# Gathered expert rows: nine buffers instead of four, rows emitted by TensorE's progress in the experts' pass, and a higher row pace beside the projections

## The chip, the cores and the metric

One core of one Trainium2 chip runs the whole program. The metric is the device time of one execution in microseconds (us). A profiled execution has a span, from its first to its last instruction, and a time of its own that is a little longer.

## The reference, cut to what matters

An encoder trunk of one layer runs over two token groups (256 and 1024 tokens, width 1024) with shared weights: retention and latent attention from one input projection, attention to 256 memory tokens, then a product-key expert layer and a last norm. The expert layer (PEER) is the part that the change touches: each token has 8 heads, each head picks 16 of 16384 experts, so 128 experts per token, and an expert is one row of U and one row of V (1024 floats each).

```python
def peer_ffn(xn, wq, sub_keys, U, V):
    def blk(xt):                                  # 128 tokens
        q = (xt @ wq).reshape(128, 8, 256)
        s1 = einsum('thd,hkd->thk', q[..., :128], sub_keys[0])
        s2 = einsum('thd,hkd->thk', q[..., 128:], sub_keys[1])
        v1, i1 = top_k(s1, 16); v2, i2 = top_k(s2, 16)
        cand = v1[..., :, None] + v2[..., None, :]        # 256 sums a head
        ts, sel = top_k(cand, 16)
        ids = take_along_axis(i1*128 + i2, sel)           # 128 experts a token
        g = softmax(ts)
        a = einsum('td,ted->te', xt, U[ids])
        return einsum('te,ted->td', g * gelu(a), V[ids])
y = rms_norm(x + peer_ffn(rms_norm(x, norm_ffn_w), ...), final_norm_w)
```

## The kernel before, in words

**Tiles and stages.** The 1280 tokens are ten tiles of 128. All work is written by one Python program, and a scheduler with a timeline model puts each engine's instructions in an order; on the chip every engine then runs its own list strictly in that order. The stages follow each other in time: the input projection with retention (`phase_a`), the first group's latent attention and its output, memory and query projections (`phase_m`, `phase_b` on tiles 0 and 1), the second group's latent attention (`phase_m`, to about 1110 us), `phase_b` on tiles 2 to 5 (to about 1440 us) and on tiles 6 to 9 (to about 1780 us), the gates (`gates`, to 2069 us), and the experts' pass (`dense`, to the end).

**Two ways to compute the experts.** Tiles 2 to 7 (`DENSE`) go through all 16384 experts on TensorE. `a_stage` loads blocks of U (`ur`), splits each into a high part on ScalarE (`uh`) and a low part on GpSimd (`ul`), and multiplies (PSUM tile `pa`, three matmuls a product); ScalarE takes the Gelu out of PSUM (`wr`), VectorE multiplies in the gates and makes the low part (`wl`); V blocks are loaded and split likewise (`vr`, `vh`, `vl`). `v_stage` multiplies into PSUM tile `pv` (two buffers) and VectorE adds it to `dacc`.

**Gathered rows.** Tiles 0, 1, 8 and 9 (`GATHER`) get only the rows they need. The generator `gather` makes, for each tile, 128 U rows and then 128 V rows. One row is an indirect DMA issued by GpSimd (line 1007) that brings 128 x 1024 floats, 0.5 MB, into a buffer of tag `grow`, of which there are four, and one VectorE instruction on it: for U a multiply with `x3` and a sum into one column of `a`, for V a multiply-add into `acc`. `banks` copies `x3` and `acc` into PSUM (tile `gps`) if the experts' pass has begun, and otherwise leaves them in SBUF (`gx`, `gacc`). 4 x 256 = 1024 rows in all.

**Where rows are put.** VectorE calls of the main work go through `Lead`, which remembers the last one as `anchor`; those of rows and of routing go through `Fill`, which gives each an ordering edge behind the current anchor: on VectorE it cannot come before it, and may come later. `tick(us)` is called beside each group of matmuls with its time at full rate. It adds that time, multiplied by a pace of `RHO`, to a debt, and takes steps of the routing generators (first) or of the gather generators until the debt is paid; a row pays 1.2 us. `RHO` has a pair (pace while routing is pending, pace of rows) for each of three stretches: the second group's attention and `phase_b`, the gates, the experts' pass. In the experts' pass the row pace is 0, and the rows left over are written after the whole pass, in the loop at the end of `run`, with the pass's beginning as anchor:

```python
            start = self.dense(sd)
            self.anchor = start
            while self.routing or self.gathering:
                self.step()
```

Of the kernel before, what the change touches and what calls it, by code (L numbers as in the profile page):

```python
# [10 lines left out]
F32 = mybir.dt.float32  # L11
F32R = mybir.dt.float32r
BF = mybir.dt.bfloat16
# [8 lines left out]
P = 128  # L22
D = 1024
# [23 lines left out]
NG = 3  # L47
O1_BY = "va"

RHO = ((0.75, 0.42), (0.5, 0.0), (0.9, 0.0))  # L50
LATE = 2


SYNC = mybir.DependencyInfo(mybir.DependencyClass.Sync, mybir.DependencyReason.DATA)
# [7 lines left out]
class Lead:  # L62


    def __init__(self, k):
        self.k = k
# [39 lines left out]
class K:  # L106
    def __init__(self, nc, tc, I, O, dbg=None):
        self.nc, self.tc, self.I, self.O = nc, tc, I, O
        self.dbg = dbg or {}
        self.n = 0  # L110
        self.routing, self.gathering = [], []
        self.keeps = []
        self.spare = ()
        self.routed = set()
        self.owed, self.rho = 0.0, (0.0, 0.0)
        self.gps = None
        self.anchor = None
        self.v, self.vf = Lead(self), Fill(self)

    def tick(self, us):  # L120


        rho = self.rho[0 if self.routing else 1]
        if self.rho is RHO[1] and self.routed.issuperset(DENSE):
            rho = 0.0
# [7 lines left out]
    def step(self, q=None):  # L133
        q = q or self.routing or self.gathering
        try:
            return next(q[0])
        except StopIteration:
            q.pop(0)
            return 0.0

    def pace(self, r, ins=None):
# [156 lines left out]
    def phase_a(self, sd):  # L298
# [3 lines left out]
        with ExitStack() as es:  # L302
# [20 lines left out]
            with ExitStack() as e2:  # L323
# [16 lines left out]
                for p in range(RH // 2):  # L340
# [9 lines left out]
                    for t in tiles:  # L350
# [12 lines left out]
                        nc.gpsimd.tensor_tensor(gg[t], gg[t], gw, ALU.mult)  # L363
                        if p and t == LATE:
                            finish()
# [620 lines left out]
    def gather(self, gp, sd, t):  # L986

        nc, I = self.nc, self.I
        v = self.vf

        def row():
            return gp.tile([P, D], F32, tag="grow", name=self.nm("grow"), bufs=4)
        ids = gp.tile([P, P], I32, tag="gids", name=self.nm("gids"), bufs=2)
        nc.sync.dma_start(ids, sd["ids"][t])
        g = gp.tile([P, P], F32, tag="gg", name=self.nm("gg"), bufs=2)
        nc.sync.dma_start(g, sd["g"][t])
        x3 = gp.tile([P, D], F32, tag="gx", name=self.nm("gx"), bufs=1)
        nc.sync.dma_start(x3, sd["x3"][t])
        fw = row()
        nc.sync.dma_start(fw, I["norm_ffn_w"].partition_broadcast(P))  # L1000
        v.tensor_tensor(x3, x3, fw, ALU.mult)
        x3 = self.banks(x3)
        a = gp.tile([P, P], F32, tag="ga", name=self.nm("ga"), bufs=2)

        def rows(src, s):
            u = row()
            nc.gpsimd.indirect_dma_start(out=u, out_offset=None, in_=src,  # L1007
                                         in_offset=bass.IndirectOffsetOnAxis(ap=ids[:, s:s + 1], axis=0))
            return u
        for s in range(P):  # L1010
            u = rows(I["peer_u"], s)
            junk = gp.tile([P, D], BF, tag="gj", name=self.nm("gj"), bufs=1)
            v.scalar_tensor_tensor(junk, u, 1.0, x3, ALU.mult, ALU.mult, accum_out=a[:, s:s + 1])
            yield 1.2
        nc.scalar.activation(a, a, AF.Gelu)
        v.tensor_tensor(a, a, g, ALU.mult)
        acc = gp.tile([P, D], F32, tag="gacc", name=self.nm("gacc"), bufs=1)
        nc.sync.dma_start(acc, sd["x2"][t])
        out, acc = acc, self.banks(acc)
        for s in range(P):  # L1020
            u = rows(I["peer_v"], s)
            v.scalar_tensor_tensor(acc, u, a[:, s:s + 1], acc, ALU.mult, ALU.add)
            yield 1.2
        w = row()
        nc.sync.dma_start(w, I["final_norm_w"].partition_broadcast(P))
        self.finish(gp, t, acc, w, gp.tile([P, D], BF, tag="gj", name=self.nm("gj"), bufs=1), out)

    def banks(self, x):

# [184 lines left out]
    def run(self):  # L1214
        nc, tc, I = self.nc, self.tc, self.I
        with ExitStack() as es:
            cp = es.enter_context(tc.tile_pool(name="const", bufs=1))
            dp = es.enter_context(tc.tile_pool(name="dram", bufs=1, space=DRAM))
            sd = {k: [dp.tile([P] + n, dt, name=f"{k}{t}") for t in range(NTILE)]
                  for k, n, dt in (("lat", [768], F32), ("mix", [512], F32), ("x1", [D], F32), ("x2", [D], F32), ("x3", [D], F32),  # L1220
                                   ("s", [16, P], F32), ("ids", [P], I32), ("g", [P], F32), ("ii", [2, P], F32))}
            sd["kv"] = [[dp.tile([P, 4, 2, MEMT], F32, name=f"kv{g}{h}") for h in range(CH)] for g in range(2)]
            sd["mixT"] = [[dp.tile([P, 4, GROUPS[g][1] * P], F32, name=f"mixT{g}{i}") for i in range(2)] for g in range(2)]
            sd["wl"] = {n: [dp.tile([KC, P, 512], F32, name=f"wl_{n}{b}") for b in range(c)]
                        for n, c in (("ca_wo", 2), ("peer_wq", 4))}
            sd["lw"] = [dp.tile([P, 5120], F32, name=f"lw{i}") for i in range(2)]
            sd["x3T"] = {t: [dp.tile([P, KC, P], F32, name=f"x3T{t}{i}") for i in range(2)] for t in DENSE}
            sd["G"] = dp.tile([HP, P, len(MADE) * P // TG, 2, TG], F32, name="G")
            self.sd = sd
            self.setup(cp)  # L1230
            def open_fill():
                self.gp = es.enter_context(tc.tile_pool(name="gp", bufs=1, side="right", reuse_waits="tile"))
                self.rp = es.enter_context(tc.tile_pool(name="rp", bufs=1, side="right", reuse_waits="tile"))
                self.i16 = self.rp.tile([P, 16], BF, name=self.nm("i16"))
                nc.scalar.dma_start(self.i16, I["iota16"])
            self.open_fill = open_fill
            self.phase_a(sd)
            self.phase_b(sd, BLOCKS[:1], lambda: self.phase_m(sd, 0, self.lw))
            self.rho = RHO[0]
            self.phase_m(sd, 1, self.lw)  # L1240
            self.mw.release()
            self.phase_b(sd, BLOCKS[1:])
            self.rho = RHO[1]
            self.dense_inputs(es.enter_context(tc.tile_pool(name="dx", bufs=1, reuse_waits="tile")))
            self.gates(sd)
            self.rho = RHO[2]
            self.gps = es.enter_context(tc.tile_pool(name="gps", bufs=1, reuse_waits="tile", space=PSUM))
            start = self.dense(sd)
            self.anchor = start
            while self.routing or self.gathering:  # L1250
                self.step()

# [73 lines left out]
```

## Time and profile before

| | us |
|---|---|
| median of 3 timed runs | 4408.38 |
| lowest and highest of them | 4407.57, 4419.09 |
| the profiled execution's own time | 4415.91 |
| its span | 4414.1 |
| its granted TensorE clock, mean | 0.968 |

The profile shows the profiled execution alone. Busy times are per engine; PE is TensorE's matmuls, PEld its weight loads, which run beside the matmul before, DVE is VectorE, ACT ScalarE, POOL GpSimd, SP the queue of the plain DMAs. A wait is put down to the event that came last before an instruction started.

### The profile page before, as it was taken

The page shows a single profiled execution, that of the slowest core. Times are in us where ns is not written, and L with a number is a line of the kernel's source. Part 1 is how long each engine was busy: PE and PEld are TensorE (multiplying, and loading weights), DVE is VectorE, ACT ScalarE, POOL GpSimd, SP SyncE. Part 2 cuts the span into 40 slices and gives each one's busy share as a digit, 9 for nine tenths or more (in the row PEclk, how much of TensorE's full clock was granted, in tenths as well). Part 3 has the DMA queues.
Part 4 walks back from the last instruction along what each step waited for, and adds up shares of the span by engine and source line. Part 5 has one row for each costly group of instructions (what it writes and reads, how often), then busy time and mean ns, then how long its engine had stood idle before and what let it go on. Part 6 is the DMA issues. An engine that isn't in the chain of part 4 may idle for free. (4 is left out here: it accounts for less than half of the span.)

```text
span 4414.1 us, 66568 instructions
## 1 busy us (share of the span) xinstructions
PE 4027.8 (91%) x23202; PEld 3574.7 (81%) x23202; DVE 3159.1 (72%) x7044; ACT 1643.1 (37%) x3570; POOL 2255.5 (51%) x2090
## 2 busy tenths in 40 slices
PE   7999888899898999777999999999999999999998
PEld 7999777667688889666888788888888888888887
DVE  5556422787566696897897777778777777777775
ACT  5333534456343343897322222222222222222223
POOL 2221243012666201676366676777776766677663
PEclk9999999899999999999999999999999999999999
DMA  2112678235778557567488898989998888898884
GB/s 88 36 41 69 210 242 279 69 92 167 249 239 303 181 184 244 169 202 226 157 267 291 279 316 307 315 304 311 317 313 302 307 291 299 303 313 304 298 296 162
DMA packets 489009, 1030.75 MB, mean 234 GB/s; under 512 B 42720, under 2 KB 201952, under 8 KB 488672
## 3 DMA queue, kind: packets, MB, share of 16 engines
q0 software_dynamic: 149536, 545.33, 35.9%
q1 hardware_dynamic: 329200, 470.66, 32.5%
q10 hardware_dynamic: 9936, 10.51, 0.7%
q8 instruction: 182, 2.98, 0.3%
q14 instruction: 155, 1.27, 0.1%
HBM read 901.87 MB, written 124.45 MB: 233 GB/s over the span
## 5 line engine op out<-in xcount | busy, mean ns | idle before, releaser
L1007 POOL DMA_INDIRECT grow<-in_peer_u,gids x512 | 529.3, 1034 | 811.2 <-DVE gj L88 251.2
L88 DVE SCALAR_TENSOR_TENSOR gps<-grow,ga,gps 128x1024 f32<-128x1024 f32 x512 | 658.0, 1285 | 209.0 <-DMA grow<-in_peer_v,gids 203.5
L164 PE MATMUL pa<-dxT,uh 128*128 128x384 f32 x2048 | 692.5, 339 | 37.5 <-ACT wr L1168 32.7
L166 PE MATMUL pa<-dxT,ul 128*128 128x384 f32 x2048 | 684.1, 339 | 7.8 <-POOL ul L1157 7.7
L165 PE MATMUL pa<-dxT,uh 128*128 128x384 f32 x2048 | 690.2, 337 | 0.0
L164 PE MATMUL pv<-vh,wh 128*128 128x512 f32 x1536 | 611.9, 401 | 77.9 <-DVE dacc L72 77.9
L1007 POOL DMA_INDIRECT grow<-in_peer_v,gids x512 | 504.5, 985 | 326.1 <-DVE gps L88 220.4
L165 PE MATMUL pv<-vl,wh 128*128 128x512 f32 x1536 | 616.2, 401 | 17.2 <-POOL vl L1181 16.8
L166 PE MATMUL pv<-vh,wl 128*128 128x512 f32 x1536 | 609.3, 397 | 0.0
L88 DVE SCALAR_TENSOR_TENSOR gj<-grow,gps 128x1024 bf16<-128x1024 f32 x384 | 467.5, 1217 | 194.0 <-DMA grow<-in_peer_u,gids 187.8
L164 PEld LDWEIGHTS pa<-dxT,uh 128*128 128x128 f32 x2048 | 387.9, 189 | 52.7 <-ACT wr L1168 36.7
L164 PEld LDWEIGHTS pv<-vh,wh 128*128 128x128 f32 x1536 | 293.7, 191 | 159.7 <-DVE dacc L72 101.8
L197 POOL TENSOR_TENSOR wl<-wraw,wh 128x512 fp32r<-128x512 f32 x180 | 240.2, 1351 | 345.0 <-ACT wh L193 264.0
L1157 POOL TENSOR_TENSOR ul<-ur,uh 128x512 fp32r<-128x512 f32 x256 | 334.3, 1310 | 155.9 <-ACT uh L1156 150.2
L166 PEld LDWEIGHTS pa<-dxT,ul 128*128 128x128 f32 x2048 | 387.1, 189 | 20.1 <-POOL ul L1157 16.7
L165 PEld LDWEIGHTS pa<-dxT,uh 128*128 128x128 f32 x2048 | 388.0, 189 | 4.3
L165 PEld LDWEIGHTS pv<-vl,wh 128*128 128x128 f32 x1536 | 294.3, 192 | 92.3 <-POOL vl L1181 37.8
L1181 POOL TENSOR_TENSOR vl<-vr,vh 128x512 fp32r<-128x512 f32 x256 | 327.2, 1296 | 67.2 <-ACT vh L1180 64.4
L166 PEld LDWEIGHTS pv<-vh,wl 128*128 128x128 f32 x1536 | 294.5, 192 | 58.0 <-DVE wl L72 0.4
L1156 ACT CAST uh<-ur 128x512 fp32r<-128x512 f32 x256 | 159.0, 621 | 485.9 <-DMA ur<-in_uT 458.4
L164 PE MATMUL pj<-act,wh 128*128 128x256 f32 x1088 | 312.1, 296 | 23.3 <-DVE ld L72 7.2
L72 DVE TENSOR_TENSOR dacc<-pv,dacc 128x1024 f32<-128x1024 f32 x258 | 311.0, 1218 | 25.8 <-PE pv L166 25.5
(282 smaller groups left out, 8969.0 us busy)
## 6 DMA issues: line engine op xcount, KB each, us to landing
ur<-in_uT SPq DMA_DIRECT2D x256, 256.0 KB, 4.0
vr<-in_peer_v SPq DMA_DIRECT2D x256, 256.0 KB, 4.1
G<-st SPq DMA_DIRECT2D x96, 512.0 KB, 6.3
gt<-G SPq DMA_DIRECT2D x64, 768.0 KB, 7.8
wraw<-in_peer_wq SPq DMA_DIRECT2D x96, 256.0 KB, 5.4
wraw<-in_w_out SPq DMA_DIRECT2D x48, 256.0 KB, 4.0
wraw<-in_ca_wq SPq DMA_DIRECT2D x48, 256.0 KB, 3.4
x<-ld SPq DMA_DIRECT2D x24, 512.0 KB, 4.8
```

Of the source, the lines that this page charges most:

```text
L72: r = f(*a, **kw)
L88: r = f(*a, **kw)
L164: mm(ps, a[0], b[0], start=first, stop=False)
L165: mm(ps, a[0], b[1], start=False, stop=False)
L166: mm(ps, a[1], b[0], start=False, stop=last)
L197: (nc.vector if self.spare and k in self.spare else eng).tensor_tensor(wl[:, :n], raw[:, :n], r32(wh[:, :n]), ALU.subtract)
L1007: nc.gpsimd.indirect_dma_start(out=u, out_offset=None, in_=src, in_offset=bass.IndirectOffsetOnAxis(ap=ids[:, s:s + 1], axis=0))
L1156: nc.scalar.copy(uh, ur)
L1157: nc.gpsimd.tensor_tensor(ul, ur, r32(uh), ALU.subtract)
L1181: nc.gpsimd.tensor_tensor(vl, vr, r32(vh), ALU.subtract)
```

## The change

In the experts' pass the row pace becomes 0.55 instead of 0, so rows are written between the matmuls' groups, with the anchor of that place; the loop at the end takes what is left. The row pace of the first stretch goes from 0.42 to 0.7. A gather that starts inside the experts' pass no longer has tags of its own for `x3` and `acc` (they are copied to PSUM): those two buffers join the ring of row buffers, and its result is written from a row buffer. When the last routing generator ends inside the pass, the routing pool `rp` is released and a pool `more` with three row buffers takes its place: 4 + 2 + 3 = 9, taken in turn.

```diff
-RHO = ((0.75, 0.42), (0.5, 0.0), (0.9, 0.0))
+RHO = ((0.75, 0.7), (0.5, 0.0), (0.9, 0.55))
+MORE = 3
...
-        self.gps = None
+        self.gps = self.rp = None
+        self.slots, self.at = ["grow"] * 4, 0
...
         except StopIteration:
             q.pop(0)
+            if self.gps is not None and not self.routing and self.rp is not None:
+
+                self.rp.release()
+                self.rp = None
+                self.more = self.tc.alloc_tile_pool(name="more", bufs=1, side="right", reuse_waits="tile")
+                self.slots += ["more"] * MORE
             return 0.0
...
+        banked = self.gps is not None
+        if banked and "gx" not in self.slots:
+            self.slots += ["gx", "gacc"]
+
         def row():
-            return gp.tile([P, D], F32, tag="grow", name=self.nm("grow"), bufs=4)
+            self.at += 1
+            tag = self.slots[self.at % len(self.slots)]
+            return (self.more if tag == "more" else gp).tile([P, D], F32, tag=tag, name=self.nm("grow"), bufs=self.slots.count(tag))
+
+        def own(tag):
+            return row() if banked else gp.tile([P, D], F32, tag=tag, name=self.nm(tag), bufs=1)
...
-        x3 = gp.tile([P, D], F32, tag="gx", name=self.nm("gx"), bufs=1)
+        x3 = own("gx")
...
-        acc = gp.tile([P, D], F32, tag="gacc", name=self.nm("gacc"), bufs=1)
+        acc = own("gacc")
...
-        self.finish(gp, t, acc, w, gp.tile([P, D], BF, tag="gj", name=self.nm("gj"), bufs=1), out)
+        self.finish(gp, t, acc, w, gp.tile([P, D], BF, tag="gj", name=self.nm("gj"), bufs=1), row() if banked else out)
...
-                self.rp = es.enter_context(tc.tile_pool(name="rp", bufs=1, side="right", reuse_waits="tile"))
+                self.rp = tc.alloc_tile_pool(name="rp", bufs=1, side="right", reuse_waits="tile")
...
             while self.routing or self.gathering:
                 self.step()
+            self.more.release()
```

## Rows read from the trace of the kernel before

**Rows 1.** Stretches: us, busy of PE, PEld, DVE, ACT, POOL; PEclk, DMA share, GB/s.
```profile
940.00:1110.00 170.00, 164.88 (x1031) 118.61 (x1029) 130.30 (x266) 101.97 (x191) 41.20 (x37) 1.00 0.48 151
1110.00:1440.00 330.00, 287.61 (x1866) 259.40 (x1866) 204.44 (x369) 127.44 (x296) 212.12 (x166) 0.94 0.80 268
1440.00:1760.00 320.00, 295.22 (x2005) 273.60 (x2006) 254.15 (x1208) 127.61 (x292) 34.74 (x30) 0.96 0.60 205
...
2200.00:4350.00 2150.00, 2025.46 (x9895) 1794.60 (x9894) 1666.03 (x2052) 540.91 (x978) 1479.90 (x1362) 0.98 0.88 301
4350.00:4406.00 56.00, 56.00 (x270) 48.86 (x268) 24.72 (x29) 19.51 (x36) 12.35 (x10) 1.00 0.21 74
```

**Rows 2.** Groups of instructions, whole run: count, busy us, mean ns, idle before.
```profile
L164 PE MATMUL pa<-dxT,uh 128*128 128x384 f32 x2048 | 692.5, 339 | 37.5 <-ACT wr L1168 32.7 <-ACT uh L1156 4.6
...
L88 DVE SCALAR_TENSOR_TENSOR gps<-grow,ga,gps 128x1024 f32<-128x1024 f32 x512 | 658.0, 1285 | 209.0 <-DMA grow<-in_peer_v,gids 203.5
...
L164 PE MATMUL pv<-vh,wh 128*128 128x512 f32 x1536 | 611.9, 401 | 77.9 <-DVE dacc L72 77.9
...
L88 DVE SCALAR_TENSOR_TENSOR gj<-grow,gps 128x1024 bf16<-128x1024 f32 x384 | 467.5, 1217 | 194.0 <-DMA grow<-in_peer_u,gids 187.8 <-ACT gps L1034 2.6 <-DVE gj L88 0.4
...
L88 DVE SCALAR_TENSOR_TENSOR gj<-grow,gx 128x1024 bf16<-128x1024 f32 x128 | 192.9, 1507 | 18.0 <-DMA grow<-in_peer_u,gids 17.1
```

**Rows 3.** Timeline of PE, 4351.9 to 4360 us: start, duration, instruction.
```profile
4351.93 0.39 PE L164 MATMUL pv<-vh,wh 128*128 128x512 f32 x1
...
4355.11 0.39 PE L166 MATMUL pv<-vh,wl 128*128 128x512 f32 x1
...
4357.20 0.33 PE L166 MATMUL pa<-dxT,ul 128*128 128x384 f32 x1
...
4359.98 0.33 PE L164 MATMUL pa<-dxT,uh 128*128 128x384 f32 x1
```

**Rows 4.** Waits of PEld, 2200 to 4406 us: us in total, times, longest.
```profile
PEld pv L164 <- DVE dacc L72: 97.8, 55, 3.9
PEld pv L165 <- POOL vl L1181: 37.8, 52, 1.9
PEld pa L164 <- ACT wr L1168: 23.9, 9, 3.5
PEld pa L166 <- POOL ul L1157: 15.1, 22, 1.0
PEld pa L164 <- ACT uh L1156: 8.1, 9, 1.3
```

**Rows 5.** Waits of DVE, 2200 to 4406 us.
```profile
DVE gps L88 <- DMA grow<-in_peer_v,gids: 203.5, 159, 5.1
DVE gj L88 <- DMA grow<-in_peer_u,gids: 187.8, 146, 4.2
```

**Rows 6.** Waits of POOL, 2200 to 4406 us.
```profile
POOL grow L1007 <- DVE gps L88: 239.0, 224, 7.3
POOL grow L1007 <- DVE gj L88: 162.2, 177, 5.6
```

**Rows 7.** Row instructions (tile grow), 2200 to 4350 us: time from issue to landing.
```profile
DMA to landing us min/median/max: 4.1/5.7/10.4
```

**Rows 8.** Stretches, row instructions alone: us, DVE busy, POOL busy, PEclk, DMA share, GB/s.
```profile
940.00:1110.00 170.00, 46.62 (x76) 41.20 (x37) 1.00 0.48 151
1110.00:1440.00 330.00, 132.66 (x156) 99.79 (x79) 0.94 0.80 268
...
2200.00:4350.00 2150.00, 1132.31 (x1283) 873.85 (x890) 0.98 0.88 301
```

**Rows 9.** Two short stretches of tiles 2 to 5, columns as in the first group.
```profile
1340.00:1400.00 60.00, 53.26 (x410) 50.95 (x409) 37.00 (x77) 18.45 (x45) 30.16 (x24) 0.94 0.95 330
1200.00:1260.00 60.00, 57.97 (x472) 57.50 (x470) 41.54 (x76) 28.52 (x75) 34.09 (x28) 0.97 0.74 236
```

**Rows 10.** Waits of DVE, 940 to 1440 us.
```profile
DVE gj L88 <- DMA grow<-in_peer_u,gids: 16.4, 6, 6.3
```

## The prediction

> **What bounds the kernel now.** I read the busy times by stretch first [rows 1]. From 2200 to 4350 us the experts' pass runs with PE busy 94% of the time, VectorE 77%, GpSimd 69% and the DMA engines 88%: half of the span in one steady state, with PE in front. PE's busy figure hides pipelined ends, so I priced the pass from the matmul counts [rows 2] and the undisturbed rhythm near the end, where nothing waits and the granted clock is 1.00 [rows 1, 3]: fourteen intervals of `pv` in 3.18 us are 0.227 us each, sixteen of `pa` in 2.78 us are 0.174. Three lines of 2048 and three of 1536 then need 6144 x 0.174 + 4608 x 0.227 = 2115 us, 0.197 us a matmul. The stretch holds 9895 of them: 1947 us of work in 2150, so about 203 us are lost.
>
> The waits of the weight loads say where [rows 4]: 98 us for `dacc` on VectorE, 53 for `vl` and `ul` on GpSimd, 24 for ScalarE's Gelu, 8 for its cast, 183 together; the rest fits a granted clock of 0.98. Who makes VectorE late? Its own waits [rows 5]: 391 us for gathered rows that have not landed. Busy and waiting together are 1666 + 391 = 2057 of 2150 us, 96%. VectorE takes its list in order, so while it stands before a row, the `dacc`, `wr` and `wl` behind it stand too, and PE with its two `pv` buffers runs dry after some 4 us (18 x 0.227 = 4.1 us a buffer). GpSimd is caught from the other side: its row DMAs stand 401 us for a buffer that VectorE has not released [rows 6], with the low parts `vl` and `ul` behind them.
>
> **Part 1, nine buffers.** The stretch holds 1283 VectorE instructions on rows [rows 8]: 384 U rows of two each (the second reads the sum out) leave some 510 for V rows [rows 2], with a few at tile changes. That is about 893 rows in 2150 us, one per 2.4 us. With four buffers a row must be issued and landed within 4 x 2.4 = 9.6 us of its buffer's release; the landing alone takes 5.7 us in the median and 10.4 at worst [rows 7], and the issue stands in GpSimd's queue before it. So about a third of the rows (305 waits) come late. With nine, there are 21.6 us, twice the worst landing. I cost VectorE's row waits at nearly nothing in the pass; what hides them is this lookahead, and if it is not used (GpSimd issuing late) the cost is the present 391 us. The first rows of the pass have six buffers, 14.4 us, until routing ends.
>
> Do the DMA engines bear it? 301 GB/s at a share of 0.88 means some 342 GB/s at full share [rows 1]. Nine buffers do not add traffic, they let it queue. The rows per us stay the same (part 2), so the pass stays under that limit.
>
> What PE gets back: VectorE falls from 96% taken to about 77%, and I let the `dacc` waits fall from 98 to 25 us and the Gelu's, which stand behind VectorE through ScalarE's list, from 24 to 10. GpSimd stays 69% busy, its splits in bursts, so `vl` and `ul` fall only from 53 to 40, the cast stays at 8. That leaves 83 of 183: **a gain of 100 us**. Bounds: 0, if the waits only change their names, and 183, if all vanish. I take a middle value, since the largest term hangs directly on the cured wait and the second does not.
>
> **Part 2, the order.** Before, rows were written after the pass and filled the scheduler's gaps. Now each group of matmuls pays 0.55 of its counted time and a row costs 1.2, so one row per 2.18 us counted. The code counts 384 or 512 columns at 2400 a us, 0.48 and 0.64 us a group of three: 2048 x 0.48 + 1536 x 0.64 = 1966 us counted in the pass. Routing of tiles 8 and 9 comes first: 35.4 us of steps each by the generators' yields, at 0.9, 79 us counted. Then 811 rows (part 3) take 811 x 2.18 = 1769. Together 1848, 94% of 1966: the rows end some 130 us before the pass, and no tail stays behind. In real time the pass would take 2115 + 83 + 20 for the clock = 2218 us, so counted us stretch by 2218/1966 = 1.13: a row per 2.46 us against 2.40: the load per us on VectorE, GpSimd and DMA is today's. I cost the order itself at 0, bounded by the number of `dacc` waits on both sides (rivals).
>
> **Part 3, pace 0.7 beside the projections.** Today 128 rows, all of tile 0's U, go there (`gj<-grow,gx`) [rows 2], 116 of them between 940 and 1440 us (76 + 156 VectorE instructions, two a row) [rows 8]. The same counted time at 0.7 gives 128 x 0.7/0.42 = 213, 85 more, and 1024 - 213 = 811 are left. The 85 are V rows of tile 0 with `acc` in SBUF.
>
> Between 940 and 1440 us VectorE is busy 130 + 204 = 335 of 500 us, 179 of them rows, 1.55 us each [rows 1, 8]. Two thirds more rows, 77, add 119 us: 454. Four buffers remain here, and the row waits, 16 us now [rows 10], may rise to what the pass shows per row, 391/893 = 0.44 us, times 193 rows = 85 us: 523 in all, over 500. At the 96% that the pass tolerated, that is 545 us, 45 more. The other side: tiles 6 to 9 run with VectorE 79% busy on routing at a PE share of 92%, better than the 87% of tiles 2 to 5 [rows 1]; so a busy VectorE alone costs nothing visible, bound 0. In between stands the DMA. Tiles 2 to 5 move 268 GB/s over 330 us, 88 MB; 50 more rows of 0.52 MB make 115 MB, 348 GB/s, full. A stretch that was nearly full (share 0.95) ran PE at 89%, one at 0.74 at 97% [rows 9]; 8% of 330 us is **26 us lost**, which I take as 25. I keep 0 to 60 for the range: the 45 and some of the weights' transfers behind rows.
>
> The released routing pool and the `x3` and `acc` buffers cost a wait at four tile changes each, some us beside other work; 0.
>
> **One rule against it.** The U rows that read `x3` from SBUF took 1507 ns in the mean, those that read it from PSUM 1217 [rows 2]. Tile 0's V rows now read and write an SBUF `acc`: 85 in the first stretch (in the 119 above) and 43 in the pass. The Trainium skill, SBUF — State Buffer, section "Who interferes with whom", says that a VectorE instruction with two SBUF inputs and a GpSimd instruction that reads SBUF exclude each other for the whole instruction. By this rule, the trace agrees: the SBUF form is the one that is stretched.
>
> **The sum.** 4415.9 - 100 + 25 = 4341 for the profiled execution, whose time stands 7.5 us above the median of the runs shown. Against that median: 4408 - 75 = **4333 us**.
>
> **The rivals.** (a) *The rows beside the projections eat the gain.* For it: rows there already move the DMA to 0.80 and VectorE would be full. Against: PE lost less at a fuller VectorE on tiles 6 to 9. At 60 lost and 60 won, 4408 us, no change. Chance 0.11.
>
> (b) *Slower: rows now written amid the pass push ahead of `dacc`.* A row is 1.29 us in front of an accumulation, and each `dacc` wait costs 98/55 = 1.8 us [rows 4]. There are 258 accumulations of which 55 make PE wait. If the even placing made 90 late, PE would lose 63 us more, and with 25 from part 3 the time is 4496. It decides from 55 waits on: with as many as today, part 3 alone makes it slower. For it: rows lose the place of gap-fillers. Against: their density is the same and the 391 us of standing are not in the schedule. Chance 0.12.
>
> (c) *The SBUF accumulator blocks GpSimd.* 43 rows of tile 0 open the pass; if each holds up a split for its own 1.29 us [rows 2], 56 us of the gain go: 4389. For it: the stretched 1507 ns. Against: only the first 5% of the pass. Chance 0.06.
>
> (d) *The change does not do what it says*: GpSimd issues rows no earlier, since its list is still timed on the last release, and the waits stay; 4408 + 25 = 4433. Against: row k + 9 needs buffer k, which is long free. Chance 0.05.
>
> (e) *Nearly all 183 us return* and part 3 costs nothing: 4225. Chance 0.06.
>
> **How the numbers follow.** The forecast has 0.60; its own range, with 60 to 140 won and 0 to 45 lost, is 4270 to 4393. I call no change what lies within 0.3%, 13 us, about the scatter of the runs shown: 4395 to 4421. Faster: 0.60 + 0.06 + 0.06 and a part of (a), 0.74. Same: the rest of (a), 0.09. Slower: (b) and (d), 0.17. The range reaches from 4262, between forecast and (e), to 4412, over (a) and (c), and leaves out (b), (d) and (e), about 0.2.
>
> **What would show it.** In the pass: VectorE's row waits far under 391 us, PE's `dacc` waits near 25, GpSimd's waits for released buffers well under 401, the last row some 130 us before the end, and matmuls at 4.8 a us instead of 4.6. Beside the projections: 85 more rows, a DMA share near 1 on tiles 2 to 5, and the gates beginning some 25 us later. I am wrong in size if the projections lose over 60 us, and wrong in kind if PE waits for `dacc` as often as now although rows no longer come late.

## The result: 41 us faster, with half of the pass's gain spent beside the projections

The changed kernel takes 4367.0 us (median of 5 runs, 4365.2 to 4381.4), the kernel before 4408.4 us (median of 5, 4403.4 to 4419.1): a ratio of 0.9911 [0.989, 0.9933]. I had forecast 4333, in a range of 4262 to 4412. The profiled execution of the changed kernel took 4367.0 us by its own time, with a span of 4365.2; against the profiled one of before (span 4414.1) the span is 48.9 us shorter. It comes in two parts. The last transposes of the gates, at whose end the experts' pass can begin, start at 2111.3 us instead of 2068.7: 42.6 us lost. From there to the last `pv` it takes 2245.2 us instead of 2336.7: 91.5 us won.

The same stretches as in [rows 1], of the changed kernel, and one in the steady middle of the pass:

```profile
940.00:1110.00 170.00, 160.59 (x992) 116.54 (x989) 149.16 (x295) 96.48 (x183) 65.43 (x60) 0.99 0.69 217
1110.00:1440.00 330.00, 274.09 (x1682) 241.89 (x1681) 217.19 (x346) 122.42 (x285) 225.85 (x174) 0.89 0.84 287
1440.00:1760.00 320.00, 280.30 (x1833) 252.71 (x1832) 286.77 (x1125) 120.85 (x276) 86.50 (x74) 0.95 0.72 244
2200.00:4300.00 2100.00, 2034.24 (x10103) 1832.13 (x10102) 1723.09 (x2152) 553.77 (x1003) 1440.43 (x1295) 0.99 0.83 291
2400.00:3900.00 1500.00, 1460.82 (x7258) 1317.50 (x7257) 1241.04 (x1513) 389.37 (x711) 1059.79 (x965) 0.99 0.86 304
```

and that middle of the kernel before, which was not shown:

```profile
2400.00:3900.00 1500.00, 1422.61 (x6982) 1267.27 (x6981) 1151.47 (x1464) 381.47 (x690) 1039.90 (x960) 0.98 0.89 305
```

In the pass PE does 7258 matmuls in 1500 us, 4.84 a us, where it did 4.65. On tiles 2 to 5 (1110 to 1440 us) it does 184 fewer than before, on tiles 6 to 9 172 fewer, though part of the second number is only that everything stands later.

The waits of the changed kernel from 2200 to 4360 us, of PE's weight loads (against [rows 4]):

```profile
PEld pv L173 <- DVE dacc L74: 46.4, 18, 4.6
PEld pv L174 <- POOL vl L1199: 18.4, 15, 4.1
PEld pa L175 <- POOL ul L1175: 13.8, 15, 2.0
PEld pa L173 <- ACT wr L1186: 5.1, 3, 3.2
PEld pa L173 <- ACT uh L1174: 3.2, 2, 2.1
```

of VectorE (against [rows 5]):

```profile
DVE wr L74 <- ACT wr L1186: 183.9, 83, 6.6
...
DVE gacc L90 <- DMA grow<-in_peer_v,gids: 5.0, 3, 3.7
...
DVE gj L90 <- DMA grow<-in_peer_u,gids: 3.1, 2, 2.0
```

and of GpSimd (against [rows 6]):

```profile
POOL grow L1025 <- DVE gps L90: 180.6, 123, 10.3
POOL grow L1025 <- DVE gj L90: 160.0, 146, 8.1
```

PE's waits are 87 us, where I had 83. VectorE's 391 us before rows that have not landed are 8 us; it now stands 184 us before ScalarE's Gelu, which follows PE. So far the prediction seems to have happened as told. The experiments show that it did not: the wait that went and the time that came are two different things.

To see where time goes by place, I compare the two traces at equal work: how many us later the changed kernel starts as many matmuls, counted from the span's start, as the kernel before has started. It is +3.2 us at 1100 us of the kernel before, +23.9 at 1440, +45.2 at 1600, +47.2 at 2400, +26.1 at 3000 and -41.7 at 4300. Half of the projections' loss is made on tiles 2 to 5, the rest at the start of tiles 6 to 9, and the pass gains steadily from about 2400 us to its end.

### The profile page after: what moved, and what is told of

It is laid out like the page before. It is cut to its first block, busy times and chain, and to the rows that moved or that the text cites. A ratio compares the mean times of both kernels' runs of the same rounds, so it can differ in the third digit from the quotient of the medians.

```text
span 4365.2 us, 66436 instructions
## 1 busy us (share of the span) xinstructions
PE 4010.5 (92%) x23202; PEld 3578.9 (82%) x23202; DVE 3281.7 (75%) x7044; ACT 1639.9 (38%) x3569; POOL 2301.6 (53%) x2090
## 4 chain that ended last, share of the span: by engine, by line
PE 26%; issue 8%; POOL 6%; DVE 6%; DMA 3%; ACT 1%; SPq 0%; POOLq 0%; ACTq 0%; DVEq 0%
PE pa L175 5%; PE pa L173 5%; PE pa L174 5%; PE pv L174 4%; PE pv L173 4%; PE pv L175 4%; POOL grow L1025 4%; DMA ur<-in_uT 2%; POOL vl L1199 1%; POOL ul L1175 1%; DVE gps L90 1%; DVE wr L74 1%; DVE dacc L74 1%; DVE wl L74 1%; DVE gj L90 1%
## 5 line engine op out<-in xcount | busy, mean ns | idle before, releaser
L1025 POOL DMA_INDIRECT grow<-in_peer_v,gids x512 | 522.5, 1020 | 545.5 <-DVE gps L90 159.9
L90 DVE SCALAR_TENSOR_TENSOR gps<-grow,ga,gps 128x1024 f32<-128x1024 f32 x384 | 493.2, 1284 | 9.6 <-ACT gps L1052 2.9
L206 POOL TENSOR_TENSOR wl<-wraw,wh 128x512 fp32r<-128x512 f32 x180 | 250.7, 1409 | 310.7 <-ACT wh L202 241.2
L74 DVE TENSOR_TENSOR wr<-wr,gt 128x384 f32<-128x384 f32 x256 | 196.2, 767 | 209.2 <-ACT wr L1186 184.2
```

Source lines behind the costliest of these rows:

```text
L74: r = f(*a, **kw)
L90: r = f(*a, **kw)
L206: (nc.vector if self.spare and k in self.spare else eng).tensor_tensor(wl[:, :n], raw[:, :n], r32(wh[:, :n]), ALU.subtract)
```

## Experiments

Theory 1 and Theory 2 in the expectations differ from run to run, and each says what it stands for. Each run had its own runs of the kernel before on the same chip (medians 4407.8, 4409.6 and 4408.0 us).

### Buffers or order: the two taken apart

The change has two parts in the pass, nine buffers and rows placed by PE's work. Three kernels fill the square, all at pace 0.7 beside the projections. The kernel before with that pace alone:

```diff
-RHO = ((0.75, 0.42), (0.5, 0.0), (0.9, 0.0))
+RHO = ((0.75, 0.7), (0.5, 0.0), (0.9, 0.0))
```

> The kernel before with only the row pace beside the projections raised from 0.42 to 0.7; the experts' pass as before (four buffers, rows written after it). Theory 1 (the parts add up): the pass begins 42 us later, as in the changed kernel, and gains only what 85 fewer rows are worth while rows run (203 us lost per 893 rows, so 85 x 0.23 = 19 us): 4408 + 42 - 19 = 4431 us. Theory 2 (moving rows forward is itself a gain): under 4408 us.

The changed kernel with its rows in the pass written after it, where no ordering edge holds them:

```diff
-RHO = ((0.75, 0.7), (0.5, 0.0), (0.9, 0.55))
+RHO = ((0.75, 0.7), (0.5, 0.0), (0.9, 0.0))
```

> The changed kernel with the row pace in the experts' pass back at 0: nine buffers, but rows written after the pass and placed by the scheduler. Theory 1 (the buffers cure VectorE's row waits, the order is worth nothing): the pass takes about what it takes in the changed kernel, 4367 +- 13 us, VectorE's row waits in the pass under 60 us. Theory 2 (the order carries the gain): row waits or waits for dacc stay at half or more of the 391 and 98 us, 4400 to 4450 us.

The changed kernel with four buffers:

```diff
-                self.slots += ["more"] * MORE
...
-            self.slots += ["gx", "gacc"]
+            pass
...
-            return row() if banked else gp.tile([P, D], F32, tag=tag, name=self.nm(tag), bufs=1)
+            return gp.tile([P, D], F32, tag=tag, name=self.nm(tag), bufs=1)
...
-        self.finish(gp, t, acc, w, gp.tile([P, D], BF, tag="gj", name=self.nm("gj"), bufs=1), row() if banked else out)
+        self.finish(gp, t, acc, w, gp.tile([P, D], BF, tag="gj", name=self.nm("gj"), bufs=1), out)
```

> The changed kernel with four row buffers only (no pool more, x3 and acc with their own buffers), rows still written by TensorE's progress at 0.55. Theory 1 (the buffers carry the gain): VectorE's row waits in the pass stay near 0.44 us a row, 350 us, PE loses 160 us or more there: 4425 to 4445 us. Theory 2 (the order carries it): near 4367 us.

| pace 0.7 beside the projections | rows after the pass, free | rows placed by PE's work |
|---|---|---|
| four buffers | 4460.3, 1.0126 [1.0102, 1.015] | 4381.1, 0.9937 [0.9914, 0.996] |
| nine buffers | 4466.5, 1.0144 [1.0119, 1.017] | 4367.0, 0.9911 [0.989, 0.9933] |

Down the left column the buffers gain nothing. Along both rows the order gains about 2%, 79 and 100 us. With the order, nine buffers are 9 to 14 us ahead of four (the changed kernel, run again, gave 4372.5), and the intervals overlap. The pass, from the gates to the last `pv`, takes 2329 and 2340 us in the left column, 2253 and 2245 in the right. The left column is slower than either theory of its two expectations: with four buffers the pass begins 50 us late and wins only 8, and with nine the row waits go as Theory 1 has it, without its gain. With four buffers and the order the time is near Theory 2's, but the row waits are Theory 1's.

All waits of PE's weight loads in the pass (from 2200 us) follow the columns too: 186 and 176 us on the left, 116 and 87 on the right, 183 in the kernel before. VectorE's waits do not. With four buffers and the order, VectorE (2200 to 4460 us) stands as long as ever before late rows:

```profile
DVE gj L90 <- DMA grow<-in_peer_u,gids: 167.4, 116, 4.7
DVE gps L90 <- DMA grow<-in_peer_v,gids: 164.8, 128, 4.7
```

332 us, and yet the pass is 84 us shorter than in the kernel before, and PE waits half as long for `dacc`. Its weight loads with four buffers (2200 to 4460 us), first with the rows free, then with the order:

```profile
PEld pv L164 <- DVE dacc L72: 92.4, 54, 5.7
```

```profile
PEld pv L172 <- DVE dacc L74: 48.6, 39, 5.6
```

With nine buffers and no order it never stands before a row, and the pass is no shorter. The stretch 2400 to 3900 us and the waits of the weight loads in it, of that kernel:

```profile
2400.00:3900.00 1500.00, 1395.24 (x6765) 1237.61 (x6763) 1326.66 (x1605) 352.93 (x667) 1124.13 (x1050) 0.97 0.94 337
```

```profile
PEld pa L175 <- POOL ul L1175: 32.3, 21, 4.5
PEld pv L173 <- DVE dacc L74: 31.0, 26, 3.4
PEld pa L175 <- issue: 26.4, 6, 5.7
PEld pv L174 <- POOL vl L1199: 25.4, 22, 2.9
```

The freed time is filled with more rows. The row instructions alone (tile `grow`, same stretch; busy of VectorE, ScalarE and GpSimd, then PEclk, DMA share, GB/s) are

```profile
2400.00:3900.00 1500.00, 920.25 (x1119) 5.86 (x10) 707.03 (x729) 0.97 0.94 337
```

729 on GpSimd, the row DMAs, against 619 in the changed kernel and 631 in the kernel before. VectorE is 88% busy, the DMA engines 94%, the last row is done at 3976 us, and the pass's last 470 us run without any row. More buffers without a limit let the rows run ahead. PE's waits for `dacc` do fall with the buffers alone, from 92 to 42 us in the pass, and those for ScalarE's Gelu from 21 to nothing. But the waits for GpSimd's low parts, which stand in its list among the row DMAs, rise from 60 to 70, those for ScalarE's casts from 13 to 29, and the profile names no cause for 26 us before matmuls that read `ul`; the sum hardly changes.

### Is it the edge, or the place in which the rows are written?

Two kernels part the ordering edge from the place in the program. In the first, rows stay where the changed kernel writes them, but each edge in the pass goes to the pass's first instruction and so orders nothing:

```diff
-            if self.k.anchor is not None:
-                self.k.tc.add_manual_dep(r.ins, self.k.anchor.name, NOSYNC, reason="pace")
+            a = self.k.hold or self.k.anchor
+            if a is not None:
+                self.k.tc.add_manual_dep(r.ins, a.name, NOSYNC, reason="pace")
...
-                    start = self.anchor
+                    start = self.hold = self.anchor
```

> The changed kernel (nine buffers, rows written at 0.55 between the matmuls' groups), but every row in the experts' pass has its ordering edge to the pass's beginning and not to the latest main instruction. Theory 1 (the ordering edges carry the gain): as the kernel with nine buffers and rows written after the pass, 4466 +- 15 us. Theory 2 (the place in the written order, that is priority, carries it): 4367 +- 15 us.

In the second, rows are written after the pass, each with the edge that the pace would have given it:

```diff
...
+        if self.rho is RHO[2] and not self.routing:
+            self.owed += us * rho
+            while self.owed > 0.0:
+                self.owed -= 1.2
+                self.marks.append(self.anchor)
+            return
...
             while self.routing or self.gathering:
+                if self.marks:
+                    self.anchor = self.marks.pop(0)
                 self.step()
```

> The changed kernel, but the rows of the experts' pass are written after the pass, each with the ordering edge that it has in the changed kernel (recorded at the pace of 0.55). Theory 1 (the edges): 4367 +- 15 us. Theory 2 (the place in the written order): 4440 us or more.

Without edges: 4486.1 us, 1.0173 [1.0151, 1.0195], 5 us above Theory 1's range, 725 row DMAs in the middle stretch, DMA share 0.93. With edges and late writing: 4375.7 us, 0.9914 [0.9891, 0.9938], 613 row DMAs, like the changed kernel. It is the edge, and not the place in the text (shown with nine buffers; with four, the two were not taken apart).

How fine must it be? A third kernel ties all rows written during one group of three blocks to the main instruction at that group's beginning:

```diff
...
             for b0 in range(0, PK, NG):
+                self.hold = self.anchor
                 cur = a_stage(b0)
```

with the same use of `hold` as above.

> The changed kernel with the rows' ordering edges in the experts' pass made coarse: each row stands behind the main instruction at the beginning of its group of three blocks (about 52 us of the pass), so the mean pace is that of the changed kernel and the place inside a group is the scheduler's. Theory 1 (the edges work as a cap on how fast rows run): 4367 to 4385 us. Theory 2 (the fine place between accumulations is what counts): 4410 us or more.

4343.0 us, 0.9856 [0.9833, 0.988]: better than the changed kernel, which ran beside it on the same chip (0.9918 [0.99, 0.9936]), and better than Theory 1 allowed. The pass takes 2217 us. PE's weight loads, 2400 to 3900 us:

```profile
PEld pa L174 <- ACT uh L1175: 12.0, 7, 2.2
PEld pv L175 <- POOL vl L1200: 8.7, 8, 3.9
PEld pv L174 <- DVE dacc L74: 5.6, 4, 3.5
```

Rows need not be spread finely; a bound on how far they may run ahead is enough. VectorE's order in some 65 instructions of the pass, from about 3200 us on (R a row, W the gates' multiply `wr`, L the low part `wl`, D a `dacc`):

```
free, nine:       DRRRRRRRRRRWRLWRLDRDRRRDRRRWLWRDLRRRRRDRWRWLRLDRRRRRRRRRWRLWRLRR
changed kernel:   LRWLRRDWLRWRLRDRRDRRRRRDRDRRRWLRWRDLRRWLRWLRRDWLRWRLRDRRDRRRRRDRD
coarse edges:     WLWDLDDRRRRRRDDRRWRLRWRLRRRRWRLRWRDLRRRRDDWLWLDRRRRRRDDRRWRLRWRL
```

Where coarse edges gain can be read: PE's waits for `dacc` in the pass (from 2200 us) are 20 us, 46 in the changed kernel, and the pass is 28 us shorter. Why stays open. A row stands between a W and its L in 119 of the changed kernel's 256 pairs and in 157 of 256 with coarse edges, so that is not it. Between 2400 and 3900 us a row stands directly before 122 of 174 accumulations in the changed kernel and before 77 of 176 with coarse edges; that this is the cause was not tested.

### The rows beside the projections

The changed kernel with the old pace there, and the pass's pace raised so that all rows still fit:

```diff
-RHO = ((0.75, 0.7), (0.5, 0.0), (0.9, 0.55))
+RHO = ((0.75, 0.42), (0.5, 0.0), (0.9, 0.58))
```

> The changed kernel with the old pace 0.42 beside the projections, and 0.58 in the experts' pass so that the 896 rows left end at 98% of it. Theory 1 (the pass has room for all rows, the projections do not): the pass begins at 2069 us and takes 10 to 25 us more than the 2246 of the changed kernel, 4335 to 4350 us in all. Theory 2 (the pass is full at its rate of rows, so what is moved into it comes back as lost time): the pass takes 40 us more or beyond, 4365 us or above, no better than the changed kernel.

The same kernel once more, beside the next two, and one with fewer rows still:

> The kernel with 0.42 beside the projections and 0.58 in the pass once more, on one chip with the changed kernel. If 0.7 beside the projections is a loss, 4349 +- 10 us and 10 us or more under the changed kernel; if the difference seen between chips was chance, within 5 us of it.

```diff
-RHO = ((0.75, 0.7), (0.5, 0.0), (0.9, 0.55))
+RHO = ((0.75, 0.2), (0.5, 0.0), (0.9, 0.62))
```

> The changed kernel with pace 0.2 beside the projections and 0.62 in the experts' pass: some 61 rows early and 963 in the pass. Theory 1 (the pass still has room): under the kernel with 0.42 and 0.58 run beside it, 4330 to 4345 us. Theory 2 (the pass is full: a row every 2.1 us takes VectorE to 0.9 and the DMA engines to 0.95): 4355 us or above.

And the changed kernel, unedited, as their yardstick:

> The changed kernel itself, beside the two other paces: 4367 +- 10 us.

| rows beside the projections | time, ratio | pass begins | pass lasts |
|---|---|---|---|
| 213 (changed, two executions) | 4367.0, 0.9911; 4372.5, 0.9918 | 2111, 2125 | 2245, 2237 |
| 128 (0.42, two executions) | 4349.2, 0.9877; 4343.9, 0.986 [0.9838, 0.9882] | 2057, 2060 | 2271, 2267 |
| 61 (0.2) | 4327.5, 0.9815 [0.9794, 0.9835] | 2039 | 2276 |

Rows are cheaper in the pass than beside the projections. From 61 to 128 early rows the pass begins some 19 us later, 0.3 us a row, and from 128 to 213 some 60 us, 0.7 us a row; taking them into the pass costs (2269 - 2241)/85 = 0.33 and (2276 - 2269)/67 = 0.1 us a row. (The rows are counted by the pace; in kernels with the same 213 early rows the pass begins at 2111 to 2125 us, so the prices are rough.) The kernel with 0.2 beats both, by 81 us against before. Its last row is done 4 us before the last `pv` starts, 100 us in the changed kernel, so at this pace the rows fill the pass to its end. Its tiles 2 to 5 (1110 to 1440 us):

```profile
1110.00:1440.00 330.00, 309.05 (x2082) 280.97 (x2081) 136.75 (x339) 138.73 (x322) 165.56 (x137) 0.97 0.68 223
```

Which resource do the early rows take from PE? I had priced VectorE and the DMA engines as alternatives, so each was lightened by itself in all of tile 0's rows: the old 128, the 85 new ones and the 43 in the pass. VectorE on 8 of 1024 columns:

```diff
+            c = slice(0, D if banked else 8)
-            v.scalar_tensor_tensor(junk, u, 1.0, x3, ALU.mult, ALU.mult, accum_out=a[:, s:s + 1])
+            v.scalar_tensor_tensor(junk[:, c], u[:, c], 1.0, x3[:, c], ALU.mult, ALU.mult, accum_out=a[:, s:s + 1])
...
-            v.scalar_tensor_tensor(acc, u, a[:, s:s + 1], acc, ALU.mult, ALU.add)
+            v.scalar_tensor_tensor(acc[:, c], u[:, c], a[:, s:s + 1], acc[:, c], ALU.mult, ALU.add)
```

> The changed kernel with VectorE's work on the rows of tile 0 cut to 8 of 1024 columns (those outputs are not the reference's); their transfers and GpSimd's issues stay. Theory 1 (the projections lose 45 us because VectorE is full): the pass begins at 2070 us or earlier, 4325 us or under. Theory 2 (because the DMA engines are full on tiles 2 to 5): the pass still begins 25 us or more after 2069, 4350 us or more.

64 of 1024 columns transferred, which VectorE then reads 16 times over:

```diff
+            if not banked:
+                nc.gpsimd.indirect_dma_start(out=u[:, 0:64], out_offset=None, in_=src.rearrange("e (a b) -> (e a) b", b=64),
+                                             in_offset=bass.IndirectOffsetOnAxis(ap=ids[:, s:s + 1], axis=0))
+                return u[:, 0:64].unsqueeze(1).broadcast_to([P, 16, 64])
...
```

> The changed kernel with the transfers of tile 0's rows cut to 64 of 1024 columns (those outputs are not the reference's); VectorE works on as many elements as before, reading the 64 columns 16 times, and GpSimd issues as many rows. Theory 1 (VectorE full): the pass still begins 25 us or more after 2069, 4350 us or more. Theory 2 (DMA engines full): 2075 us or earlier, 4325 us or under.

Tiles 2 to 5 with little VectorE work:

```profile
1110.00:1440.00 330.00, 295.40 (x1929) 266.05 (x1929) 133.41 (x409) 129.67 (x302) 210.83 (x196) 0.93 0.91 321
```

and with little transfer:

```profile
1110.00:1440.00 330.00, 282.77 (x1758) 251.46 (x1759) 265.99 (x400) 123.71 (x287) 266.84 (x198) 0.91 0.49 152
```

The first took 4300.0 us (0.9748 [0.9727, 0.9768]), with the pass beginning at 2075 us, 6 later than in the kernel before. At equal work it is 8 us ahead of that kernel at 1440 us, though its DMA engines are at 0.91, above the changed kernel's 0.84. The second took 4344.5 us (0.9853 [0.9833, 0.9873]); it is 19 us late at 1440, 10 at 1800, and also begins the pass at 2075. (At its end the first is ahead also because tile 0's V rows in the pass are light.)

The first does not show that transfers are free, since the 128 old rows are light in it too: VectorE is busy 133 us on tiles 2 to 5, 204 in the kernel before. The kernel with 0.2 has VectorE as lightly loaded there (137 us, 58 of them rows in both) and the DMA share at 0.68, with 39 row DMAs against 106. It does 2082 matmuls against 1929, is 27 us ahead of the kernel before at 1440 us, and begins the pass 36 us sooner. So full transfers, with their issues on GpSimd, cost 19 us on tiles 2 to 5 beside a light VectorE.

Against the changed kernel, VectorE's work off tile 0's rows gives back 32 us by 1440 us and 36.6 by the pass's beginning; the transfers off the same rows give back 5 and 36.3, and that although VectorE is then busier on tiles 2 to 5 (266 us against 217), since more rows pass there (116 row DMAs against 93). Both resources cost, about alike by the gates. Neither theory holds alone. GpSimd's issues are in both kernels; what they cost was not tested by itself.

## Why the prediction was right, and the step of it that failed

**The size and the place came out as forecast, the parts did not.** PE's waits in the pass fell from 183 to 87 us (83 forecast), the pass won 92 (100), 212 rows ran early (213), matmuls go at 4.84 a us (4.8), and VectorE's row waits went. The last row ends some 100 us before the pass (130). But the 83 was met by luck: the `dacc` waits fell to 46 us and not near 25, and the low parts to 32 (40), the Gelu to 5 (10) and the cast to 3 (8) made up for it. A time of 4367 stands inside the range, 34 us above the forecast: 18 of them are part 3, 8 the pass, and 7.5 come from the profiled execution of before, which stood that much above its median, while that of the changed kernel is the median.

**Part 1 gave the gain to the wrong cause.** "I let the `dacc` waits fall from 98 to 25 us ... since the largest term hangs directly on the cured wait": the term does fall with the cure, but PE's waits as a whole do not hang on it. The row waits can go and PE gets nothing back (nine buffers, rows free: 176 us of waits), and they can stay at 332 us and PE's waits still fall (four buffers with the order: 116 us). Busy and waiting together at 96% had made VectorE look like an engine without slack; as I read these runs, a wait in its list costs PE nothing when nothing behind it is due. What the buffers give once the order is there is 9 to 14 us, not resolved.

**Part 2 is the failed step: "I cost the order itself at 0".** The order is worth about 2%, the whole gain, and the experiment that takes only its edges away is 119 us slower than the changed kernel. That the time fell into the range is therefore in part luck: a gain of about the forecast size came from a term put at nothing. My bounds for them were there (the number of `dacc` waits on both sides), but I took the middle because the rows per us stay the same. They stay the same only thanks to the edges: at nine free buffers the scheduler packs 729 rows in 1500 us instead of 619. With four buffers the rows per us hardly differ (629 free, 613 in order) and the order still gains 79 us, and PE's waits for `dacc` fall from 92 to 49; which property of the order does it there remains open.

**GpSimd.** "GpSimd's waits for released buffers well under 401" was wrong: [rows 6] became 341, and in longer single waits. Nine buffers fill up too when the rows' issue is ahead of VectorE; GpSimd then waits for a ninth buffer as it did for a fourth. It cost PE little: its waits for `vl` and `ul` fell from 53 to 32 us.

**Part 3 was too small: 25 us forecast, 42.6 measured.** Tiles 2 to 5 alone came out nearly as priced: 21 us, from +3.2 at 1100 us to +23.9 at 1440. Left out was the start of tiles 6 to 9, where rows from the end of the pace's share still run, with another 21 by 1600: row instructions there take 75 us of VectorE between 1440 and 1760 us, 15 before. The reasons for the 25 were wrong in kind. The "DMA share near 1 on tiles 2 to 5" did not come; it rose from 0.80 to 0.84, with 93 row DMAs there instead of 79, where some 50 more were forecast. The price by DMA share fails: with VectorE's work off the rows the share is 0.91, and 32 us come back by 1440. And "a busy VectorE alone costs nothing visible" fails against 19 us with hardly any transfer. The upper bound was also added up wrongly: 454 us busy and 85 us of waits are 539 and not 523, since the 16 us of old waits are in no busy time, and at 96% that is 61 us more and not 45.

**The rivals.** (a) is the nearest: the early rows ate 43 of 92 us, not all. (b) did not come: the `dacc` waits fell from 55 to 18 times. Without edges its time, 4496, is about what was measured, 4486 and 4467, but not by its mechanism: `dacc` made PE wait 39 and 33 times there, fewer than before. Those kernels are slow because the pass begins 50 and 43 us late and wins nothing back. (c) The accumulator in SBUF shows, and costs nothing visible. Groups of VectorE from 900 to 2420 us, and further down the same two operations with PSUM over the whole run:

```profile
L90 DVE SCALAR_TENSOR_TENSOR gacc<-grow,ga,gacc 128x1024 f32<-128x1024 f32 x128 | 193.7, 1513 | 32.7 <-DMA grow<-in_peer_v,gids 31.3
L90 DVE SCALAR_TENSOR_TENSOR gj<-grow,gx 128x1024 bf16<-128x1024 f32 x128 | 177.1, 1384 | 30.8 <-DMA grow<-in_peer_u,gids 29.9
```

```profile
L90 DVE SCALAR_TENSOR_TENSOR gps<-grow,ga,gps 128x1024 f32<-128x1024 f32 x384 | 493.2, 1284 | 9.6 <-ACT gps L1052 2.9
L90 DVE SCALAR_TENSOR_TENSOR gj<-grow,gps 128x1024 bf16<-128x1024 f32 x384 | 466.7, 1215 | 11.2 <-DMA grow<-in_peer_u,gids 3.1
```

1513 against 1284 ns and 1384 against 1215. The rule of the Trainium skill, SBUF — State Buffer, section "Who interferes with whom", that two SBUF inputs on VectorE and a GpSimd instruction that reads SBUF exclude each other, agrees with these rows. The overlaps in time show it more sharply: over the whole run 41 of these 128 V rows overlap a GpSimd TENSOR_TENSOR and take 2016 ns in the mean, the other 87 take 1277 and none over 1287; of the 128 U rows 25 overlap and take 2065, the other 103 take 1218. PE hardly felt it in the pass: at its opening the changed kernel falls at most 6 us further behind (+42.5 at 2200 us, +48.0 at 2300, +47.2 at 2400). Beside the projections the lengthening may be part of what VectorE's work costs; that was not taken apart. (d) and (e) did not come.

## What to carry to other kernels

A wait that an engine spends in front of filler work (work put into the gaps of the main work, here the rows) need not be time that the bounding engine loses; before a cure for it is priced, look whether anything that the bounding engine needs is overdue behind it, and try the cure and the order apart. Filler work under a scheduler wants a cap tied to the progress of the engine that sets the end: here a coarse one, one edge for each group of blocks, was enough and better than a fine one (0.9856 against 0.9918). And work that is moved is priced at both ends: 0.3 to 0.7 us a row beside the projections, 0.1 to 0.33 in the pass, so that moving rows out of the projections (pace 0.2 and 0.62) gave the best kernel with the reference's outputs, 4327.5 us; coarse edges with that pace were not tried.

## What the runs showed of the hardware that I had not expected

What a DMA share costs PE cannot be read from the share alone. At 0.91 and 321 GB/s for 330 us, with VectorE busy 133 us, PE did 1929 matmuls; at 0.84 and 287 GB/s, with VectorE busy 217 us, 1682; at 0.68 and 223 GB/s, with VectorE busy 137 us, 2082. I had taken 0.95 as a price by itself.

TensorE's granted clock moved with how well it was fed on tiles 2 to 5: 0.97 in the kernel with 2082 matmuls there, 0.94 with 1866 [rows 1], 0.89 with 1682; each is a mean over its two levels, 1.2 and 2.4 GHz. With tile 0's rows lightened it was 0.93 (1929 matmuls) and 0.91 (1758). So part of the 21 us lost there may be a lower clock; how much of it was not taken apart.

Nine rows in flight did not slow the single row much: from issue to landing, in the pass of the changed kernel, against [rows 7]:

```profile
DMA to landing us min/median/max: 3.0/6.0/11.6
```
